# The attention's reciprocal: a power on GpSimd instead of logarithm, exponential and Newton step

## The chip, the core and the metric

The kernel runs on one core of a Trainium2 chip. The core has five engines that run side by side and meet through semaphores: TensorE (PE; its weight loads are shown as PEld), VectorE (DVE), ScalarE (ACT), GpSimd (POOL) and SyncE (SP), which issues nearly all transfers here. Every engine works through its own instructions in a fixed order. The metric is device time in microseconds (us) from the first to the last instruction, with what lies around it.

## The reference

One encoder layer is applied to two requests, a prompt of 1024 tokens and a sample of 256, each behind 16 learned meta tokens. The input is normalised and projected by one matrix of 2048 x 6656; the strips of 128 columns are queries, keys, values and gates of 16 heads. Eight heads attend to all tokens (two heads of keys and values for the eight), eight to a neighbourhood and the meta tokens. Each head's output is multiplied by a gate, and one matrix of 2048 x 2048 projects the result back. The part that the change touches is the softmax:

```
s = jnp.einsum('blkgd,bskd->bkgls', qg, k).astype(jnp.float32) * scale
p = jax.nn.softmax(s, axis=-1).astype(v.dtype)
o = jnp.einsum('bkgls,bskd->blkgd', p, v)
...
ya = global_gqa(qa, ka, va) * jax.nn.silu(za)
```

The softmax divides each exponential by the sum over the keys. The kernel divides at the end: it sums the products of unnormalised exponentials and values, and multiplies by the gate and by one over the sum.

## The kernel before, in words

All matrix products are made of three passes in a reduced 32-bit format: each operand is split into a high part (a cast on ACT, L52) and a low part (a subtraction on DVE, L53), and high x high, high x low and low x high are added in PSUM.

The work has three stages. The first chunk (`chunk1`) projects 512 tokens (meta, sample and the first 240 of the prompt) strip by strip in `strips` (L178 to L180) and does the attention of the sample: 16 blocks of 256 queries, one per head. The second chunk (`chunk2`) projects the other 784 tokens and does the attention of the prompt: 32 wide blocks (`attend`: 256 queries against all 1024 keys, L300 to L302 for the scores and L340 to L343 for the values), and 32 narrow ones (`attend_strip`: L405 to L407 and L436 to L439). The last narrow blocks lie beside the first steps of the output projection (`outproj`, `products`, L887 to L889).

A block goes like this. Keys lie along the partitions, queries along the free dimension. PE makes the scores; ACT and DVE copy them to SBUF and take the running maximum (L304 to L315); `all_max` adds the meta scores (L250) and has POOL take the maximum over the partitions (`ma`, L252); DVE subtracts it (L320), ACT takes the exponential (L321), both split it for PE; `all_sum` adds up (L267), and POOL sums over the partitions (`tot`, L269): afterwards each of the 128 partitions holds the same 256 sums. PE multiplies by the values into `po`. Then `put_y` makes `y`: the reciprocal `r` of `tot` (L276 to L279), `po` times the gate (L282 or L285), that times `r` (L286), and the store to `yd` from SP (L287). The product with the gate, which frees the one PSUM buffer of `po`, doesn't need `r`.

POOL's other work is the sum over the partitions for the queries' and keys' norms (`m`, L188 in `qk_evac`), which the evacuation of a projected strip waits for. Four PSUM buffers (`pp`) hold projected strips.

Between the blocks the projections run on: the next heads' strips, and strips for the narrow heads that are done ahead (`fill`). The order in which each engine takes its instructions is written out when the kernel is built, by a planner that simulates the program and issues what is ready by priority (`TileContext(..., schedule_with_timeline_sim=True)`); weight loads have a raised priority (`woff`) and run ahead, in rings of three raw and four split buffers. Only after the attention, from step 8 of `outproj`, the order is that of the program (`in_order`). At run time the order is fixed: an instruction that waits holds all that stands behind it on its engine.

The reciprocal before is an estimate and one Newton step: exp(-ln(tot)) on ACT, then on DVE `tot * r`, and `(tot * r - 2) * r`, which is minus the refined reciprocal; the sign is taken back in L286 by a factor of -1.

Of the kernel before, what the change touches and what calls it, by code (L numbers as in the profile page):

```python
# [12 lines left out]
F32 = mybir.dt.float32  # L13
F32R = mybir.dt.float32r
AF = mybir.ActivationFunctionType
ALU = mybir.AluOpType
# [4 lines left out]
P = 128  # L21
# [13 lines left out]
QB = 256  # L35
# [10 lines left out]
class Kern:  # L46
# [225 lines left out]
    def put_y(self, po, tot, zs, ydst):  # L272

        nc = self.nc
        r = self.t.tile([P, QB], F32, tag="t", name="r")
        nc.scalar.activation(r[:], tot[:], AF.Ln)  # L276
        nc.scalar.activation(r[:], r[:], AF.Exp, scale=-1.0)
        nc.vector.tensor_tensor(out=tot[:], in0=tot[:], in1=r[:], op=ALU.mult)
        nc.vector.scalar_tensor_tensor(out=r[:], in0=tot[:], scalar=2.0, in1=r[:], op0=ALU.subtract, op1=ALU.mult)  # L279
        y = self.y.tile([P, QB], F32, tag="y", name="y")  # L280
        if len(zs.shape) == 3:
            nc.vector.tensor_tensor(out=y[:].rearrange("p (g r) -> p g r", g=4), in0=po[:].rearrange("p (g r) -> p g r", g=4),  # L282
                                    in1=zs, op=ALU.mult)
        else:
            nc.vector.tensor_tensor(out=y[:], in0=po[:], in1=zs, op=ALU.mult)  # L285
        nc.vector.scalar_tensor_tensor(out=y[:], in0=y[:], scalar=-1.0, in1=r[:], op0=ALU.mult, op1=ALU.mult)  # L286
        nc.sync.dma_start(ydst, y[:].rearrange("p (g r) -> p g r", g=4) if len(ydst.shape) == 3 else y[:])  # L287

    def attend(self, q, zs, keys, meta, vals, vmeta, ydst):
# [700 lines left out]
    def build(self):  # L990
        tc, nc, io = self.tc, self.nc, self.io
        self.woff = 300
        nc.scalar.preload_act_table_set("natural_log_exp_and_others")
        with tc.tile_pool(name="dr", bufs=1, space=DRAM) as dp, tc.tile_pool(name="const", bufs=1) as cp, \
                tc.tile_pool(name="raw", bufs=3) as self.raw, tc.tile_pool(name="w", bufs=4) as self.w:
            self.kd = [dp.tile([P, 2, NMETA + C1P], F32, name=f"kd{g}") for g in range(10)]
            self.vn = [dp.tile([NP, P], F32, name=f"vn{g}") for g in range(10)]
            self.vmd = [dp.tile([M3, P], F32, name=f"vmd{g}") for g in range(10)]
            self.qd = [dp.tile([P, 2, C1P], F32, name=f"qd{h}") for h in range(16)]
            self.zd = [dp.tile([P, NP], F32, name=f"zd{h}") for h in range(16)]  # L1000
            self.k2d = [dp.tile([P, T2], F32, name=f"k2d{g}") for g in range(10)]
            self.q2d = [dp.tile([P, T2], F32, name=f"q2d{h}") for h in range(16)]
            self.yd = [dp.tile([P, NP + NS], F32, name=f"yd{h}") for h in range(16)]
            self.x2d = [dp.tile([P, T2], F32, name=f"x2d{k}") for k in range(KT)]
            self.wld = [dp.tile([P, KT, P], F32, name=f"wld{c}") for c in range(52)]
            self.td = [{p: dp.tile([P, 8, P], F32, name=f"td{c}_{p}") for p in (5, 6, 7, 4)} for c in range(8)]
            self.ident = cp.tile([P, P], F32, name="ident")
            make_identity(nc, self.ident)
            self.nw = cp.tile([P, KT], F32, name="nw")
            self.nqkw = cp.tile([P, 4], F32, name="nqkw")  # L1010
            self.qkw = cp.tile([P, 4], F32, name="qkw")
            with ExitStack() as ps, ExitStack() as es_y:
                def pool(stack, name, bufs, **kw):
                    setattr(self, name, stack.enter_context(tc.tile_pool(name=name, bufs=bufs, **kw)))

                for name, bufs in (("sp", 2), ("op", 1), ("tp", 1)):
                    pool(ps, name, bufs, space=PSUM)
                es_pp, es_x, es_attn, es_proj, es_late = (ExitStack() for _ in range(5))
                kw = {"reuse_waits": "tile"}
                pool(es_pp, "pp", 4, space=PSUM)  # L1020
                pool(ps, "mt", 1)
                self.meta_tiles()
                work = (("s", 5), ("ph", 2), ("sm", 2), ("mx", 2), ("t", 6))
                raw = self.raw
                with ExitStack() as es_1:
                    pool(es_1, "x", 16, side="right")
                    for name, bufs in (("raw", 5), ("tab", 1), ("k", 1), ("v", 1), *work, ("y", 2), ("one", 1), ("ev", 9), ("xr", 10)):
                        pool(es_1, name, bufs)
                    self.chunk1()
                self.raw = raw  # L1030
                pool(es_x, "x", 16, side="right", **kw)
                for name, bufs in (("one", 1), ("ev", 8)):
                    pool(es_proj, name, bufs, side="right", **kw)
                for name, bufs in (("k", 1), ("v", 1), ("tab", 1), ("q", 1), ("z", 1), *work, ("y", 1)):
                    pool(es_attn, name, bufs, **kw)
                self.chunk2()
                es_proj.close()
                es_x.close()
                es_pp.close()
                pool(es_y, "pq", 2, space=PSUM, **kw)  # L1040
                for name, bufs in (("ym", 16), ("us", 8)):
                    pool(es_late, name, bufs, side="right", **kw)
                self.raws, self.ws = [self.raw] * 2, [self.w] * 2

                def end_attention():
                    es_attn.close()
                    for name, bufs in (("yr", 4), ("ysp", 1), ("w2", 4), ("raw2", 4), ("vs", 8), ("ob", 3)):
                        pool(es_y, name, bufs, **kw)
                    self.raws[1], self.ws[1] = self.raw2, self.w2
                    self.ysum = [self.ysp.tile([P, TH], F32, tag=f"ys{k}", name="ysum") for k in range(8)]  # L1050

                self.outproj(end_attention)
                es_late.close()
# [70 lines left out]
```

## Time and profile before

| | us |
|---|---|
| three runs, median | 2243.62 (2240.49 to 2244.88) |
| the profiled execution | 2239.06 |
| its span, first to last instruction | 2237.3 |
| busy: PE | 2203.6 |
| busy: DVE | 1636.4 |
| busy: ACT | 1128.8 |
| busy: POOL | 524.8 |

The profile is that of one execution, taken by the hardware profiler. A group row reads: line, engine, operation, tiles written and read, shape, count, then the busy time in us and the mean duration in ns, and behind the second bar the idle time of the engine just before, and what ended it. A row of the timeline reads: start and duration in us, engine, line, operation, tiles, count, and in brackets the idle time before. A row of a stage reads: its bounds and length, the busy time (and number) of each engine, the granted TensorE clock as a share of full speed, the share of the transfer engines, and GB/s.

### The profile page before, as it was taken

The page shows a single profiled execution, that of the slowest core. Times are in us where ns is not written, and L with a number is a line of the kernel's source. Part 1 is how long each engine was busy: PE and PEld are TensorE (multiplying, and loading weights), DVE is VectorE, ACT ScalarE, POOL GpSimd, SP SyncE. Part 2 cuts the span into 40 slices and gives each one's busy share as a digit, 9 for nine tenths or more (in the row PEclk, how much of TensorE's full clock was granted, in tenths as well). Part 3 has the DMA queues.
Part 4 walks back from the last instruction along what each step waited for, and adds up shares of the span by engine and source line. Part 5 has one row for each costly group of instructions (what it writes and reads, how often), then busy time and mean ns, then how long its engine had stood idle before and what let it go on. Part 6 is the DMA issues. An engine that isn't in the chain of part 4 may idle for free.

```text
span 2237.3 us, 36770 instructions
## 1 busy us (share of the span) xinstructions
PE 2203.6 (98%) x13074; PEld 2091.4 (93%) x13074; DVE 1636.4 (73%) x2895; ACT 1128.8 (50%) x2297; POOL 524.8 (23%) x249
## 2 busy tenths in 40 slices
PE   8999999999969999999999999999999999999999
PEld 7888788888869999999999999999999999999999
DVE  8687876677665899886898889767668776636743
ACT  6555544444464667665666666444344454232220
POOL 1232421222102243221233223323223312000000
PEclk9999999999989999999999999999999999999999
DMA  8767899976454333334333345644334464845663
GB/s 295 218 193 229 288 328 335 300 237 199 137 189 131 104 110 110 104 109 138 105 105 103 106 120 159 201 150 144 116 114 132 134 200 146 262 145 162 201 209 111
DMA packets 262873, 384.80 MB, mean 172 GB/s; under 512 B 46208, under 2 KB 121888, under 8 KB 262688
## 3 DMA queue, kind: packets, MB, share of 16 engines
q1 hardware_dynamic: 262688, 382.44, 54.2%
q8 instruction: 103, 1.69, 0.3%
q14 instruction: 82, 0.67, 0.1%
HBM read 279.77 MB, written 102.42 MB: 171 GB/s over the span
## 4 chain that ended last, share of the span: by engine, by line
PE 86%; DVE 6%; DMA 4%; ACT 2%; issue 1%; POOL 1%; SPq 0%; DVEq 0%; POOLq 0%; ACTq 0%
PE pp L179 18%; PE pp L180 18%; PE pp L178 18%; PE pq L887 6%; PE pq L889 6%; PE pq L888 6%; PE po L439 2%; PE sp L300 1%; PE sp L302 1%; PE sp L301 1%; PE po L342 1%; PE po L341 1%; PE po L340 1%; DVE wl L53 1%; DMA wld<-wl 1%
## 5 line engine op out<-in xcount | busy, mean ns | idle before, releaser
L179 PE MATMUL pp<-x,wh 128*128 128x392 f32 (+2 forms) x2496 | 894.5, 359 | 10.6 <-DVE x L130 10.6
L178 PE MATMUL pp<-x,wh 128*128 128x392 f32 (+2 forms) x2496 | 893.9, 359 | 5.9 <-ACT wh L52 5.9
L180 PE MATMUL pp<-x,wl 128*128 128x392 f32 (+2 forms) x2496 | 892.1, 358 | 0.2 <-DVE wl L53 0.2
L179 PEld LDWEIGHTS pp<-x,wh 128*128 128x128 f32 x2496 | 470.2, 188 | 42.7 <-DVE x L130 11.1
L178 PEld LDWEIGHTS pp<-x,wh 128*128 128x128 f32 x2496 | 469.5, 188 | 38.7 <-ACT wh L52 7.3
L180 PEld LDWEIGHTS pp<-x,wl 128*128 128x128 f32 x2496 | 470.1, 188 | 32.8 <-DVE wl L53 1.2
L53 DVE TENSOR_TENSOR wl<-wr,wh 128x512 fp32r<-128x512 f32 (+1 forms) x402 | 291.1, 736 | 141.9 <-ACT wh L52 94.4
L52 ACT CAST wh<-wr 128x512 fp32r<-128x512 f32 (+1 forms) x402 | 239.7, 609 | 228.7 <-PE pp L179 168.8
L188 POOL PARTITION_ALL_REDUCE m<-ms x78 | 227.1, 2911 | 362.9 <-ACT ms L186 327.8
L269 POOL PARTITION_ALL_REDUCE tot<-a x80 | 188.4, 2354 | 459.6 <-DVE a L267 436.6
L888 PE MATMUL pq<-ym,wh 128*128 128x320 f32 x896 | 277.4, 310 | 0.3 <-DVE ym L53 0.3
L889 PE MATMUL pq<-ym,wl 128*128 128x320 f32 x896 | 277.4, 310 | 0.0
L887 PE MATMUL pq<-ym,wh 128*128 128x320 f32 x896 | 277.2, 310 | 0.0
L252 POOL PARTITION_ALL_REDUCE ma<-m x80 | 100.7, 1259 | 460.8 <-DVE m L250 458.4
L888 PEld LDWEIGHTS pq<-ym,wh 128*128 128x128 f32 x896 | 168.4, 188 | 0.6 <-DVE ym L53 0.6
L887 PEld LDWEIGHTS pq<-ym,wh 128*128 128x128 f32 x896 | 168.2, 188 | 0.1
L889 PEld LDWEIGHTS pq<-ym,wl 128*128 128x128 f32 x896 | 168.4, 188 | 0.0
L320 DVE TENSOR_TENSOR S<-S,ma 128x512 f32<-128x512 f32 x136 | 105.4, 830 | 8.8 <-POOL ma L252 8.5
L53 DVE TENSOR_TENSOR pl<-S,ph 128x512 fp32r<-128x512 f32 x136 | 98.0, 727 | 13.4 <-ACT ph L52 13.0
L59 ACT ACTIVATE rs_l<-m 128x392 f32<-128x392 f32 (+2 forms) x78 | 43.9, 562 | 126.7 <-DVE m L189 125.1
L304 ACT COPY S<-sp 128x512 f32<-128x512 f32 x136 | 78.1, 578 | 51.4 <-PE sp L302 38.9
L321 ACT ACTIVATE S<-S 128x512 f32<-128x512 f32 x136 | 83.9, 629 | 39.7 <-DVE S L320 39.3
(207 smaller groups left out, 3338.1 us busy)
## 6 DMA issues: line engine op xcount, KB each, us to landing
wr<-in_w_in SPq DMA_DIRECT2D x414, 256.0 KB
wld<-wl SPq DMA_DIRECT2D x132, 256.0 KB
wl<-wld SPq DMA_DIRECT2D x132, 256.0 KB
wq<-in_w_out SPq DMA_DIRECT2D x64, 256.0 KB
td<-wq SPq DMA_DIRECT2D x64, 256.0 KB
wr<-td SPq DMA_DIRECT2D x64, 256.0 KB
yr<-yd SPq DMA_DIRECT2D x48, 320.0 KB
wr<-in_w_out SPq DMA_DIRECT2D x48, 256.0 KB
```

The source lines that it names most:

```text
L52: nc.scalar.copy(hi, full)
L53: return nc.vector.tensor_tensor(out=lo, in0=full, in1=hi.bitcast(F32), op=ALU.subtract).ins
L178: nc.tensor.matmul(p[:, :n], wh[:, k, :], xh[:, o:o + n], start=first, stop=False)
L179: nc.tensor.matmul(p[:, :n], wh[:, k, :], xl[:, o:o + n], start=False, stop=False)
L180: nc.tensor.matmul(p[:, :n], wl[:, k, :], xh[:, o:o + n], start=False, stop=last)
L188: nc.gpsimd.partition_all_reduce(m2[:], ms[:], P, RED.add)
L252: nc.gpsimd.partition_all_reduce(ma[:], m1[:], P, RED.max)
L269: nc.gpsimd.partition_all_reduce(tot[:], a1[:], P, RED.add)
L320: nc.vector.tensor_tensor(out=s, in0=s, in1=mb, op=ALU.subtract)
L887: nc.tensor.matmul(ps[:, b, :B], wh, yh[:, o], start=k == 0, stop=False)
L888: nc.tensor.matmul(ps[:, b, :B], wh, yl[:, o], start=False, stop=False)
L889: nc.tensor.matmul(ps[:, b, :B], wl, yh[:, o], start=False, stop=k == 7)
```

## The change

The reciprocal becomes one instruction on POOL: `tot` to the power of -1, where the exponents come from a new constant column `m1` of -1.0 that is read again for each of the 256 columns. The two ACT passes and the two DVE passes of the estimate and the Newton step go. Since `r` now has its true sign, the last multiplication is a plain product of two tensors on DVE. All 80 blocks use `put_y`.

```diff
         nc = self.nc
         r = self.t.tile([P, QB], F32, tag="t", name="r")
-        nc.scalar.activation(r[:], tot[:], AF.Ln)
-        nc.scalar.activation(r[:], r[:], AF.Exp, scale=-1.0)
-        nc.vector.tensor_tensor(out=tot[:], in0=tot[:], in1=r[:], op=ALU.mult)
-        nc.vector.scalar_tensor_tensor(out=r[:], in0=tot[:], scalar=2.0, in1=r[:], op0=ALU.subtract, op1=ALU.mult)
+        nc.gpsimd.tensor_tensor(out=r[:], in0=tot[:], in1=self.m1[:].to_broadcast([P, QB]), op=ALU.pow)
         y = self.y.tile([P, QB], F32, tag="y", name="y")
...
             nc.vector.tensor_tensor(out=y[:], in0=po[:], in1=zs, op=ALU.mult)
-        nc.vector.scalar_tensor_tensor(out=y[:], in0=y[:], scalar=-1.0, in1=r[:], op0=ALU.mult, op1=ALU.mult)
+        nc.vector.tensor_tensor(out=y[:], in0=y[:], in1=r[:], op=ALU.mult)
         nc.sync.dma_start(ydst, y[:].rearrange("p (g r) -> p g r", g=4) if len(ydst.shape) == 3 else y[:])
...
             make_identity(nc, self.ident)
+            self.m1 = cp.tile([P, 1], F32, name="m1")
+            nc.gpsimd.memset(self.m1[:], -1.0)
```

## The prediction

> **What bounds the kernel now.** I read the page first: the engines' busy time and the chain that ended last.
>
> ```profile
> span 2237.3 us, 36770 instructions
> PE 2203.6 (98%) x13074; PEld 2091.4 (93%) x13074; DVE 1636.4 (73%) x2895; ACT 1128.8 (50%) x2297; POOL 524.8 (23%) x249
> ...
> PE 86%; DVE 6%; DMA 4%; ACT 2%; issue 1%; POOL 1%; SPq 0%; DVEq 0%; POOLq 0%; ACTq 0%
> ```
>
> TensorE (PE) is busy for 2203.6 of 2237.3 us, so at most 33.7 us could be won by taking work off the other engines. What matters is whether the edit makes PE wait. The next view is the busy time by stage: the 16 small attention blocks of the first chunk (88 to 634 us), two runs of 16 wide blocks (`attend`, one per group of heads, 740 to 1056 and 1080 to 1396), and the narrow blocks (`attend_strip`, 1396 to 1890).
>
> ```profile
> core 0: us, PE busy (x) PEld busy (x) DVE busy (x) ACT busy (x) POOL busy (x), PEclk, DMA share, GB/s
> 88.00:634.00 546.00, 536.98 (x2535) 446.21 (x2533) 393.27 (x673) 266.63 (x537) 147.27 (x56) 1.00 0.77 247
> 740.00:1056.00 316.00, 316.00 (x2052) 315.11 (x2051) 274.02 (x494) 207.06 (x430) 88.45 (x43) 1.00 0.38 111
> 1080.00:1396.00 316.00, 315.31 (x2059) 312.47 (x2058) 283.90 (x515) 209.47 (x438) 99.74 (x48) 1.00 0.38 116
> 1396.00:1890.00 494.00, 492.68 (x3074) 491.06 (x3074) 357.43 (x724) 230.74 (x499) 150.37 (x82) 1.00 0.46 145
> ```
>
> PE has no gap in any of the attention stages. VectorE (DVE) is the next fullest: 274.0 of 316 us (87%) in the wide stage, 72% elsewhere. The third view is POOL (GpSimd) in order of time, in the wide stage.
>
> ```profile
> 1083.37 1.06 POOL L252 PARTITION_ALL_REDUCE ma<-m  x1 [0.58 <-DVE m L250]
> 1096.30 1.79 POOL L269 PARTITION_ALL_REDUCE tot<-a  x1 [11.86 <-DVE a L267]
> 1100.50 1.06 POOL L252 PARTITION_ALL_REDUCE ma<-m  x1 [2.42 <-DVE m L250]
> ```
>
> The blocks run one behind the other, 17.1 us apart here: the reduction for the maximum (`ma`), 11.9 us of exponentials and sums, the reduction for the sum (`tot`), and 2.4 us after its end the next block's `ma`. The new power reads `tot`, so it lands in exactly that short gap of POOL. And the chain of waits, in order of time, goes through `ma` in this stage:
>
> ```profile
> 1134.74 2.73 POOL ma L252
> 1137.49 4.01 DVE S L320 x4
> ```
>
> So a late `ma` there is not covered: PE's work is in a fixed order, and the next score and value products stand in it.
>
> **The change, part by part.** Removed from each of the 80 calls of `put_y`: two ACT passes and two DVE passes.
>
> ```profile
> L279 DVE SCALAR_TENSOR_TENSOR r<-tot,r 128x256 f32<-128x256 f32 x80 | 35.5, 444 | 1.3
> ...
> L278 DVE TENSOR_TENSOR tot<-tot,r 128x256 f32<-128x256 f32 x80 | 34.8, 435 | 28.0 <-ACT r L277 27.1
> ...
> L276 ACT ACTIVATE r<-tot 128x256 f32<-128x256 f32 x80 | 33.3, 416 | 84.8 <-POOL tot L269 84.5
> L277 ACT ACTIVATE r<-r 128x256 f32<-128x256 f32 x80 | 33.2, 415 | 1.7
> ```
>
> That frees 33.3 + 33.2 = 66.5 us of ACT and 35.5 + 34.8 = 70.3 us of DVE (0.88 us a block). Neither is what PE waits for, so I count the gain as 0. L286 stays with a plainer opcode and the same operands: 0. The memset of `m1` happens once, like the `vm` memset of 0.2 us at the start: 0.
>
> Added: 80 powers of 128x256 on POOL, an operation that no row shows. The nearest rows are POOL's plain passes:
>
> ```profile
> L488 POOL MEMSET Pm<- x2: 314/316/317, 0.9 to 1.1; 128x256 f32 x2
> ```
>
> ```profile
> 9.79 1.23 POOL masks.py:199 TENSOR_SCALAR_AFFINE_SELECT ident<-ident 128x128 f32<-128x128 f32 x1 [8.22 <-issue]
> ```
>
> One pass over 128x256 costs 0.316 us if it only writes; the select, which tests and chooses, costs 1.23 us for half the elements, 2.46 us for all. A full-precision power is a logarithm, a product and an exponential. If POOL does these by arithmetic and not by a table, I count some 32 steps (split off the exponent 3, polynomial 8, product in two words 6, split off the integer 2, second polynomial 6, put the exponent back 2, special values 5). At one pass each that is 32 x 0.316 = 10.1 us, the price I take: the operation is nearer to a string of passes than to a single one. The ends: 2.5 us (the select) below, and 64 passes or 20 us above.
>
> [...] No run here shows a two-input POOL pass.
>
> What waits: DVE's `y` multiply (L286) waits for the power, and behind it on DVE stand the splits of weights, the projections' evacuations and the next block's maximum; the `yd` store (L287) waits on SP with the weight loads and rope shuffles behind it. The weights are loaded ahead and hide it; the maximum and the shuffles are part of the same lateness that I charge now. POOL itself runs in order, so `ma` and the projections' reductions (L188) start only when the power is done. How much of the 10.1 us fits in the gaps, from POOL's groups in the wide stage (x16), the narrow one (x31) and the first chunk (two rows):
>
> ```profile
> L252 POOL PARTITION_ALL_REDUCE ma<-m x16 | 20.4, 1277 | 53.1 <-DVE m L250 53.1
> ```
>
> ```profile
> L252 POOL PARTITION_ALL_REDUCE ma<-m x31 | 37.6, 1212 | 133.3 <-DVE m L250 130.9 <-DMA wr<-in_w_in 2.2
> ```
>
> ```profile
> L188 POOL PARTITION_ALL_REDUCE m<-ms x24 | 79.3, 3302 | 115.9 <-ACT ms L186 91.6 <-DMA wld<-wl 10.3 <-DMA wr<-in_w_in 7.9
> L252 POOL PARTITION_ALL_REDUCE ma<-m x16 | 21.5, 1341 | 225.1 <-DVE m L250 225.1
> ```
>
> - Wide: 53.1 / 16 = 3.3 us idle before `ma` (where a reduction L188 comes first, that one is late instead). Each block is late by 10.1 - 3.3 = 6.8 us; 32 x 6.8 = 218 us.
> - Narrow: 133.3 / 31 = 4.3 us idle; late by 5.8 us. Here PE comes later to the value product than its input is ready:
>
> ```profile
> 1494.95 0.41 ACT L261 CAST Pm<-Sm 48x256 fp32r<-48x256 f32 x1
> ```
>
> ```profile
> 1499.31 0.34 PE L178 MATMUL pp<-x,wh 128*128 128x392 f32 x1
> 1499.49 0.34 PE L179 MATMUL pp<-x,wh 128*128 128x392 f32 x1
> 1499.66 0.38 PE L460 MATMUL tp<-ident,vt 128*128 128x128 f32 x2
> 1499.80 0.36 PE L436 MATMUL po<-Pm,vm 128*128 128x256 f32 x1
> ```
>
>   The probabilities end at 1495.36, the product starts at 1499.80: 4.4 us of cover. 32 x (5.8 - 4.4) = 45 us.
> - First chunk: 225.1 / 16 = 14.1 us idle before `ma`, more than 10.1: 0. A reduction L188 has 115.9 / 24 = 4.8 us; late by 5.3 us, 16 x 5.3 = 85 us at most. I take 0, since four PSUM buffers stand between it and PE, and keep 85 for the range.
> - Clock: after the idle stretch at the change of chunks PE ran at half clock (0.55 in the mean of the first window), with 0.33 us from matmul to matmul where the rows at 1499 us have 0.18.
>
> ```profile
> 649.03 0.53 PE L180 MATMUL pp<-x,wl 128*128 128x392 f32 x1
> 649.36 0.53 PE L179 MATMUL pp<-x,wh 128*128 128x392 f32 x1
> ```
>
> ```profile
> 648.00:652.00 4.00, 3.46 (x12) 3.46 (x13) 4.00 (x7) 3.18 (x9) 0.00 (x0) 0.55 0.00 0
> 652.00:656.00 4.00, 4.00 (x24) 4.00 (x24) 4.00 (x6) 1.89 (x4) 0.00 (x0) 1.00 0.00 0
> ```
>
>   Up to 3.4 us at half clock lose 1.7 us per long stall; for half of the 32 wide blocks 16 x 1.7 = 27 us.
>
> Sum: the profiled execution took 2239.06 us (the median of the runs is 4.6 us higher, 0.2%); 2239 + 218 + 45 + 27 = 2529, forecast **2530 us**. With a power of 6 us it is 2239 + 32 x 2.7 = 2325; with 13 us, 2239 + 32 x 9.7 + 32 x 4.3 + 27 = 2714.
>
> **The rivals.**
>
> *The power is short and fits in the gap* (the other side). It decides at 3.3 us. For it: the select at 2.46 us for all elements. Against: the select does one test, the power dozens of steps. Then nothing is late, and the freed DVE and ACT time can only shorten PE's 33.7 us of waits, mostly at the change of chunks: 2236 us.
>
> *The power also holds DVE.* DVE passes with two inputs in SBUF are held while a POOL reduction runs; those with one input in PSUM never are:
>
> ```profile
> L320 DVE TENSOR_TENSOR S<-S,ma x136: 675/684/2669, 95.0 to 1373.1; 128x512 f32<-128x512 f32 x136
> ```
>
> ```profile
> L310 DVE TENSOR_TENSOR mx<-mx,sp x64: 666/680/691, 736.6 to 1362.4; 128x512 f32<-128x512 f32 x64
> ```
>
> ```profile
> 366.49 3.24 POOL L188 PARTITION_ALL_REDUCE m<-ms  x1 [7.87 <-DMA wr<-in_w_in]
> ```
>
> ```profile
> 366.64 3.39 DVE L510 TENSOR_TENSOR wq<-wq 128x512 f32<-128x512 f32 x2
> ```
>
> L320 (two in SBUF) reaches 2669 ns, L310 (one in PSUM) never passes 691; two passes at L510 took 3.39 us inside a 3.24 us reduction. If a power holds DVE for its whole 10.1 us, DVE is the bound: 274 - 14 + 16 x 10.1 = 422 us of work in a wide stage of 316, so +106, and +116 in the second; 357 - 27 + 31 x 10.1 = 643 in 494 narrow, +149; in the first chunk 541 fits in 546. 2239 + 371 + 27 = 2637 us, and 2870 us at 13 us a power. Against: a reduction held L510 for only about 2 of its 3.24 us, and the power may read its input early.
> [...]
>
> *The power is far dearer*: 20 us, or code fetched at each switch from reduction to power (POOL sat 8.22 us in "issue" before its first select; no reduction shows that). 32 x 16.7 + 32 x 11.3 + 16 x 5.9 + 54 = 1044, so 3283 us.
>
> **How the numbers follow.** Forecast (power 6 to 13 us, POOL's queue late) 0.50, its own range 2325 to 2715; power between 3.3 and 6 us, 2240 to 2325, 0.06; short power 0.12; DVE held 0.24; far dearer 0.08. Leaving out the short and the far dearer power (0.20 together), and taking in the 85 us of the first chunk and DVE held with 13 us, the range is 2270 to 3000. A measurement of this kernel can tell about 0.2%, 4.5 us, from no change. Only the short power gives that: within 0.2% 0.09, faster 0.03, slower 0.88.
>
> **What would show it.** In the profile after: the duration of the new POOL group (10 us; under 3.3 us the forecast falls); `ma` starting right behind the power in the wide stage; PE below 95% busy between 740 us and the end of the wide blocks, with waits on DVE and ACT at L300 and L340, and a granted clock under 1.0 there. If L320 or L53 lengthen to the power's own duration, the held DVE is right. If the power is long and PE still full, the wide blocks had cover that I did not see.

## The result, and the profile after

The changed kernel takes 5911.74 us (median of 4 runs, 5909.94 to 5913.47); the kernel before took 2242.09 us beside it (4 runs, 2240.49 to 2244.88). The ratio is 2.636, with a 95% interval of 2.632 to 2.641. The forecast was 2530 us in a range of 2270 to 3000: the direction was right, the size was not, and even the dearest rival (3283 us) stayed far below.

The page of the changed kernel: busy time, three rows of tenths in 40 slices, and the chain that ended last.

```profile
span 5910.1 us, 36754 instructions
...
PE 2458.6 (42%) x13074; PEld 2293.3 (39%) x13074; DVE 1587.8 (27%) x2735; ACT 1094.4 (19%) x2137; POOL 3777.6 (64%) x330
...
PE   9353545667414261414323665456010100100399
...
POOL 3767656556766676666666767777767677776500
PEclk9676777878657685657666777778555555555699
...
POOL 27%; PE 9%; issue 8%; DVE 3%; POOLq 1%; ACT 1%; DMA 0%; SPq 0%; DVEq 0%; ACTq 0%
```

PE falls from 98% busy to 42%, and POOL is the fullest engine with 64%. In the last third of the attention PE works for less than a tenth of most slices. Only the last two slices, the output projection without a reciprocal, look as before. The chain names POOL first, and next to PE something that it calls "issue": time in which the engine waited for nothing that the profile shows. The costliest groups of the same page say who waits:

```profile
L276 POOL TENSOR_TENSOR r<-tot,m 128x256 f32<-128x256 f32 x80 | 3296.8, 41210 | 593.9 <-issue 482.9
...
L283 DVE TENSOR_TENSOR y<-y,r 128x256 f32<-128x256 f32 x80 | 34.0, 425 | 2725.5 <-POOL r L276 2725.5
L433 PE MATMUL po<-Pm,vm 128*128 128x256 f32 x32 | 17.7, 552 | 1509.1 <-DVE Pm L262 1179.0
...
L337 PE MATMUL po<-ph,va 128*128 128x256 f32 x256 | 102.6, 401 | 1220.8 <-ACT ph L52 1220.8
```

(The lines of code after `put_y` stand three lower than before.) One power takes 41.2 us. That alone is four times the price in the forecast. Behind the bar stand 593.9 us of idle POOL time in front of the 80 powers, 7.4 us each, most of it (482.9 us) put down to "issue". PE waits in the value products of the narrow blocks (1509.1 us) and the wide ones (1220.8 us), for probabilities that come late. One wide block on POOL, in order of time:

```profile
1368.51 2.17 POOL L269 PARTITION_ALL_REDUCE tot<-a  x1 [10.95 <-DVE a L267]
1377.71 41.17 POOL L276 TENSOR_TENSOR r<-tot,m 128x256 f32<-128x256 f32 x1 [7.04 <-issue]
1424.90 1.08 POOL L252 PARTITION_ALL_REDUCE ma<-m  x1 [6.01 <-issue]
1425.90 2.65 POOL L188 PARTITION_ALL_REDUCE m<-ms  x1
1438.05 1.79 POOL L269 PARTITION_ALL_REDUCE tot<-a  x1 [9.51 <-DVE a L267]
```

The blocks are 69.5 us apart (1368.51 to 1438.05) where they were 17.1. There is a hole of 7.0 us ahead of the power and one of 6.0 us behind it, though the sum was there, and the next maximum's input too, since 1371.74 us by DVE's timeline:

```profile
1371.33 0.41 DVE L250 TENSOR_TENSOR m<-m,Sm 16x256 f32<-16x256 f32 x1
```

What stands in these holes is in the list of all the instructions that line 276 gave POOL and its sequencer (count, then duration in ns: least, median, most):

```profile
L276 POOLq MODIFY_POOL_CONFIG  x160: 87/88/88, 108.0 to 5513.3; - x160
L276 POOL TENSOR_TENSOR r<-tot,m x80: 41172/41172/41813, 115.7 to 5524.1; 128x256 f32<-128x256 f32 x80
```

Ahead of each power stand two instructions that by their name change POOL's configuration (MODIFY_POOL_CONFIG), and ahead of the reduction behind it two more (122 at L252, 34 at L188, 2 at L138). They last 0.1 us each at most, but a hole of 6 to 7 us follows them (the first starts at 108.0 us, the first power at 115.7); what fills it the profile doesn't show. So a power costs 7.4 + 41.2 + 6.0 = 54.6 us of POOL, and 80 of them 4368 us. In the kernel before there are four such instructions in the whole program, two at 1.6 us and two at 11.2 us.

The stages, between two landmarks that both kernels have: the first wide block's `ma`, and the last `tot`. First the kernel before, a row of POOL's timeline and one of the list of L269:

```profile
743.57 1.06 POOL L252 PARTITION_ALL_REDUCE ma<-m  x1 [0.58 <-DVE m L250]
```

```profile
L269 POOL PARTITION_ALL_REDUCE tot<-a x80: 1793/2092/5072, 100.9 to 1883.6; - x80
```

Then the same two rows of the changed kernel:

```profile
1356.23 1.33 POOL L252 PARTITION_ALL_REDUCE ma<-m  x1 [1.24 <-DVE m L250]
```

```profile
L269 POOL PARTITION_ALL_REDUCE tot<-a x80: 1794/1872/3453, 104.6 to 5511.5; - x80
```

| | before | after | difference |
|---|---|---|---|
| start to the first wide `ma` | 743.6 | 1356.2 | +613 |
| first wide `ma` to the last `tot` | 1140.0 | 4155.3 | +3015 |
| last `tot` to the end | 353.7 | 398.6 | +45 |

### The profile page after: what moved, and what is told of

Same layout as the page of the kernel before. It is cut to its first block, busy times and chain, and to the rows that moved or that the text cites. A ratio compares the mean times of both kernels' runs of the same rounds, so it can differ in the third digit from the quotient of the medians.

```text
span 5910.1 us, 36754 instructions
## 1 busy us (share of the span) xinstructions
PE 2458.6 (42%) x13074; PEld 2293.3 (39%) x13074; DVE 1587.8 (27%) x2735; ACT 1094.4 (19%) x2137; POOL 3777.6 (64%) x330
## 5 line engine op out<-in xcount | busy, mean ns | idle before, releaser
L276 POOL TENSOR_TENSOR r<-tot,m 128x256 f32<-128x256 f32 x80 | 3296.8, 41210 | 593.9 <-issue 482.9
L178 PE MATMUL pp<-x,wh 128*128 128x392 f32 (+2 forms) x2496 | 915.8, 368 | 321.3 <-DVE rs_r L204 301.2
L179 PE MATMUL pp<-x,wh 128*128 128x392 f32 (+2 forms) x2496 | 912.7, 366 | 2.5 <-DVE x L130 2.5
L180 PE MATMUL pp<-x,wl 128*128 128x392 f32 (+2 forms) x2496 | 907.0, 364 | 0.2 <-DVE wl L53 0.2
L283 DVE TENSOR_TENSOR y<-y,r 128x256 f32<-128x256 f32 x80 | 34.0, 425 | 2725.5 <-POOL r L276 2725.5
L433 PE MATMUL po<-Pm,vm 128*128 128x256 f32 x32 | 17.7, 552 | 1509.1 <-DVE Pm L262 1179.0
L178 PEld LDWEIGHTS pp<-x,wh 128*128 128x128 f32 x2496 | 483.6, 194 | 361.9 <-issue 283.6
L337 PE MATMUL po<-ph,va 128*128 128x256 f32 x256 | 102.6, 401 | 1220.8 <-ACT ph L52 1220.8
L337 PEld LDWEIGHTS po<-ph,va 128*128 128x128 f32 x256 | 73.8, 288 | 1229.8 <-ACT ph L52 1229.6
L179 PEld LDWEIGHTS pp<-x,wh 128*128 128x128 f32 x2496 | 483.8, 194 | 36.0 <-DVE x L130 2.7
L269 POOL PARTITION_ALL_REDUCE tot<-a x80 | 160.6, 2008 | 396.4 <-DVE a L267 396.4
L252 POOL PARTITION_ALL_REDUCE ma<-m x80 | 88.4, 1105 | 492.4 <-issue 353.5
L188 POOL PARTITION_ALL_REDUCE m<-ms x78 | 225.9, 2896 | 264.1 <-ACT ms L186 136.0
L53 DVE TENSOR_TENSOR wl<-wr,wh 128x512 fp32r<-128x512 f32 (+1 forms) x402 | 275.7, 696 | 418.6 <-ACT wh L52 399.3
```

The source lines that it names most:

```text
L53: return nc.vector.tensor_tensor(out=lo, in0=full, in1=hi.bitcast(F32), op=ALU.subtract).ins
L178: nc.tensor.matmul(p[:, :n], wh[:, k, :], xh[:, o:o + n], start=first, stop=False)
L179: nc.tensor.matmul(p[:, :n], wh[:, k, :], xl[:, o:o + n], start=False, stop=False)
L180: nc.tensor.matmul(p[:, :n], wl[:, k, :], xh[:, o:o + n], start=False, stop=last)
L188: nc.gpsimd.partition_all_reduce(m2[:], ms[:], P, RED.add)
L269: nc.gpsimd.partition_all_reduce(tot[:], a1[:], P, RED.add)
```

## The experiments

The first theory: POOL's own queue is late by the price of the power with its changes of configuration. That price has two parts, arithmetic and change, and the experiments take them apart, along with the question of who stands in the queue. Each diff is against the kernel before, unless it says otherwise; the column `m1` is there in all. The times of e6 and e7 are medians of 11 and 4 runs; every other experiment was run once.

**e1_mult: the changes without the arithmetic.** Against the changed kernel:

```diff
-        nc.gpsimd.tensor_tensor(out=r[:], in0=tot[:], in1=self.m1[:].to_broadcast([P, QB]), op=ALU.pow)
+        nc.gpsimd.tensor_tensor(out=r[:], in0=tot[:], in1=self.m1[:].to_broadcast([P, QB]), op=ALU.mult)
```

> The power is replaced by a product of the same two tensors on POOL, so the output lacks the reciprocal. Theory (every plain two-tensor operation between two reductions makes POOL change its code twice, and POOL's queue carries it to PE): the new row falls from 41.2 us to under 1 us, 160 MODIFY_POOL_CONFIG rows stay at it, about 13.6 us of switching a block stays, and by the prediction's formula with a price of 14.2 us the time is 2239 + 32 x 10.9 + 32 x 5.5 + about 40 = 2800 us. Rival (only the power needs other code): no such rows, time 2235 to 2260 us.

Measured: 2928.18 us (the kernel before beside it 2237.88), 128 us above the theory's 2800 and far from its rival. POOL's group for the product:

```profile
L276 POOL TENSOR_TENSOR r<-tot,m 128x256 f32<-128x256 f32 x80 | 48.3, 604 | 615.4 <-issue 562.6 <-DMA wld<-wl 20.6 <-DMA z<-zd 14.2
```

The product takes 0.6 us, and there are 7.7 us of idle time ahead of it all the same. An operation that lasts 0.6 us makes the kernel 690 us slower. The changes of configuration are a price of their own, and the product between the reductions pays it as the power does.

**e2_mult_unread and e3_pow_unread: the same operations, with nobody waiting.** The old reciprocal stays; behind the Newton step POOL overwrites `tot`, which nobody reads any more:

```diff
         nc.vector.scalar_tensor_tensor(out=r[:], in0=tot[:], scalar=2.0, in1=r[:], op0=ALU.subtract, op1=ALU.mult)
+        nc.gpsimd.tensor_tensor(out=tot[:], in0=tot[:], in1=self.m1[:].to_broadcast([P, QB]), op=ALU.mult)   # e3: ALU.pow
```

> The old reciprocal is back; behind it a product on POOL overwrites tot, and nothing reads it. Theory (POOL's queue: the next reductions stand behind the switching): the same lateness as with the product read, 2700 to 2850 us. Rival (the loss comes from DVE, which waits for POOL at the y multiply and holds what stands behind it): nobody waits any more, 2240 to 2350 us.

> The same with the power: the old reciprocal feeds y, and a power that nothing reads follows on POOL. Theory (POOL's queue): 5800 to 5950 us, as with the change. Rival (DVE's wait at the y multiply adds its own part): down to what POOL alone needs, 80 x 54.7 + 476 us of reductions + about 430 us outside the attention = 5280 us.

Measured: 2732.7 us with the product, 5369.5 us with the power. So most of the loss is there without a reader of the result: it comes from POOL's queue, from what stands behind the operation. But e3 missed the theory's 5800 to 5950 us and landed near the rival's floor. POOL's timeline of e3 shows a difference that I hadn't counted on:

```profile
1301.94 1.81 POOL L269 PARTITION_ALL_REDUCE tot<-a  x1 [5.84 <-issue]
1303.66 2.65 POOL L188 PARTITION_ALL_REDUCE m<-ms  x1
1306.21 1.15 POOL L252 PARTITION_ALL_REDUCE ma<-m  x1
1314.66 41.17 POOL L280 TENSOR_TENSOR tot<-tot,m 128x256 f32<-128x256 f32 x1 [7.30 <-DVE rs_r L202]
1362.13 2.57 POOL L188 PARTITION_ALL_REDUCE m<-ms  x1 [6.29 <-issue]
1364.62 1.88 POOL L269 PARTITION_ALL_REDUCE tot<-a  x1
```

Here the planner put the power behind the next block's `ma`, so that the exponentials between that `ma` and its `tot` run beside the power, and `tot` needs no wait of its own. In the changed kernel the power stands right behind its own `tot`, and the next `ma`, exponentials and `tot` come one after the other behind it. Counted over both timelines, the power comes directly behind a `ma` 60 times of 80 in e3, and never in the changed kernel, where it comes directly behind a `tot` 69 times. The 542 us between 5912 and 5370 could be this place, or DVE standing at the multiply that reads the power; the last two runs tell these apart.

**e5_pow64 and e10_pow_half_rows: what the arithmetic is paid by.** In e5 the power does 64 of the 256 columns on all 128 partitions, in e10 all 256 columns on 64 partitions; the rest goes the old way:

```diff
+        c = 64
+        nc.gpsimd.tensor_tensor(out=r[:, :c], in0=tot[:, :c], in1=self.m1[:].to_broadcast([P, c]), op=ALU.pow)
+        nc.scalar.activation(r[:, c:], tot[:, c:], AF.Ln)
...
```

> The power on 64 of the 256 columns, the old way for the other 192. Theory (the price goes by the column, 41.2/256 = 0.161 us each): 10.3 us a power, 23.9 us with the switching, and by the prediction's formula 2239 + 32 x 20.6 + 32 x 15.2 + 16 x 9.8 + 54 = 3595 us. Rival (a fixed price of an instruction): about 41 us a power and 5900 us.

> The power on 64 of the 128 partitions, all 256 columns; the other 64 partitions the old way. Theory (the price goes by the column, whatever the number of partitions): 41.2 us a power, 5800 to 6000 us. Rival (by the element): 20.6 us a power, 34 us with the switching, and by the prediction's formula 2239 + 32 x 30.8 + 32 x 25.4 + 16 x 20 + 54 = 4410 us.

Measured: e5 3564.3 us, e10 5906.81 us. POOL's group of e5, and the list of L277 in e10:

```profile
L277 POOL TENSOR_TENSOR r<-tot,m 128x64 f32<-128x64 f32 x80 | 848.0, 10600 | 610.8 <-issue 474.9 <-DMA wld<-wl 35.5 <-DMA vn<-vl 22.3
```

```profile
L277 POOL TENSOR_TENSOR r<-tot,m x80: 41172/41173/41707, 112.0 to 5518.3; 64x256 f32<-64x256 f32 x80
```

A quarter of the columns takes 10.6 of 41.2 us, half of the partitions takes the same 41.2 us. The power costs 0.161 us for each column (41.17 / 256), with 64 partitions as with 128. And e5, whose arithmetic of 10.6 us is near the price that the forecast took, can be put into the forecast's formula: with 7.6 + 10.6 + 6.0 = 24.2 us it gives 2239 + 32 x 20.9 + 32 x 15.5 + 16 x 10.1 = 3565 us without its clock term.

**e4_pow3: three powers in a row.**

```diff
+        nc.gpsimd.tensor_tensor(out=r[:], in0=tot[:], in1=self.m1[:].to_broadcast([P, QB]), op=ALU.pow)
+        nc.gpsimd.tensor_tensor(out=r[:], in0=r[:], in1=self.m1[:].to_broadcast([P, QB]), op=ALU.pow)
+        nc.gpsimd.tensor_tensor(out=r[:], in0=r[:], in1=self.m1[:].to_broadcast([P, QB]), op=ALU.pow)
```

> Three powers in a row instead of one (the reciprocal of the reciprocal of the reciprocal). Theory (a switch comes with each change between reduction and plain operation, not with each power): still 160 MODIFY_POOL_CONFIG rows at the power's lines, a price of 3 x 41.2 + 13.5 = 137 us a block, and by the prediction's formula 2239 + 32 x 133.7 + 32 x 128.3 + 16 x 123 + 54 = 12650 us. Rival (each power brings its own switches): 480 rows and over 14700 us.

Measured: 12885.45 us, 2% above the theory's number, but not by the theory's order. The lists of the three lines show 4, 158 and 158 configuration instructions ahead of the powers, 320 where 160 were expected. POOL's timeline tells why:

```profile
3104.32 1.81 POOL L269 PARTITION_ALL_REDUCE tot<-a  x1 [5.75 <-issue]
3113.52 41.17 POOL L278 TENSOR_TENSOR r<-r,m 128x256 f32<-128x256 f32 x1 [7.40 <-issue]
3154.69 41.11 POOL L276 TENSOR_TENSOR r<-tot,m 128x256 f32<-128x256 f32 x1
3201.56 1.08 POOL L252 PARTITION_ALL_REDUCE ma<-m  x1 [5.76 <-issue]
```

One block's third power (L278) and the next block's first (L276) stand back to back, without a hole; the others have a reduction between them. So the hole belongs to the alternation of reduction and elementwise operation, not to the power: two of a kind in a row pay nothing. That the total met the expectation is chance. With two pairs of changes a block the price is 3 x 41.2 + 2 x 13.4 = 150.4 us, and the formula gives 2239 + 32 x 147.1 + 32 x 141.7 + 16 x 136.3 = 13661 us, 6% too much. In e4 POOL hardly waits for anything else: its busy time on the page, 10343.7 us, and 160 pairs of holes at 13.4 us make 12488 of the 12885 us.

**e6_none and e7_dve_recip: what the removed passes are worth.** e6 multiplies by `tot` itself and has no reciprocal at all; e7 has one reciprocal instruction on DVE:

```diff
-        (the two activations, the product and the Newton step)
+        nc.vector.reciprocal(out=r[:], in_=tot[:])      # e7; nothing in e6
```

> No reciprocal at all: the two ACT and two DVE passes go and nothing comes instead, y is multiplied by tot itself, so the output lacks the reciprocal. Theory (the removed passes were beside PE's work, gain 0): 2235 to 2245 us. Rival (they cost PE something): under 2230 us.

> DVE's own reciprocal, one instruction, in place of the power. A candidate for a version better than both. It keeps POOL free; DVE has 0.88 us a block less of the old passes and one reciprocal more, of unknown duration. Theory (what counts is whether PE waits): with 2 us or less DVE still fits in the wide stage (274 - 14 + 32 = 292 of 316 us), 2235 to 2260 us. Rival (DVE's order is tight in the wide stage, so each us more is late there): 32 x 1.2 = 38 us more, 2280 us.

Measured: e6 2242.99 us, a ratio to before of 1.0012 (1.0003 to 1.0021); e7 2261.35 us, 1.0098 (1.0082 to 1.0113). Without any reciprocal the kernel is not faster, so by this run another way of making it has nothing to gain. The reciprocal on DVE takes 1.75 us, twice the two passes that it replaces there, and costs 1%, a little more than its theory's 2260 us:

```profile
L276 DVE RECIPROCAL r<-tot 128x256 f32<-128x256 f32 x80 | 139.8, 1748 | 30.0 <-POOL tot L269 30.0
```

**e8_y_on_pool and e9_mult_y_on_pool: the reader moved to POOL.** If DVE's wait at the last multiply were what costs, POOL could do that multiply itself. e8 against the changed kernel; e9 is the same with e1's product for the power:

```diff
-        nc.vector.tensor_tensor(out=y[:], in0=y[:], in1=r[:], op=ALU.mult)
+        nc.gpsimd.tensor_tensor(out=y[:], in0=y[:], in1=r[:], op=ALU.mult)
```

> As the change, but the last multiplication by r is on POOL, right behind the power: DVE no longer waits for the power, and POOL has one more plain product (0.6 us) a block, with no further switch. Theory (of the time of the change, what the unread power took away, 5912 - 5370 = 542 us, is DVE's queue standing behind that multiplication): 5370 + 80 x 0.6 = 5420 us, 5350 to 5500. Rival (it is the old reciprocal being placed elsewhere by the planner, or y being late): 5850 to 5980 us.

> The same with the product in place of the power (the output lacks the reciprocal). Theory (DVE's queue): the 195 us between the product that is read and the one that isn't go, 2733 + 48 = 2780 us, 2700 to 2830. Rival: 2900 to 3000 us.

Measured: e8 6546.01 us, e9 3338.88 us. Both are above both theories, so they do not decide the question. POOL's timeline of e8 shows what got in the way:

```profile
1556.75 1.08 POOL L252 PARTITION_ALL_REDUCE ma<-m  x1 [6.04 <-issue]
1557.75 2.65 POOL L188 PARTITION_ALL_REDUCE m<-ms  x1
1567.70 0.73 POOL L283 TENSOR_TENSOR y<-y,r 128x256 f32<-128x256 f32 x1 [7.30 <-issue]
1574.32 1.81 POOL L269 PARTITION_ALL_REDUCE tot<-a  x1 [5.90 <-issue]
```

The multiply was placed behind the next reductions and not behind the power, and pays a second pair of changes. The lists count 160 configuration instructions ahead of the powers (in e9, the products) and these ahead of the multiplies, in e8 and in e9:

```profile
L283 POOLq MODIFY_POOL_CONFIG  x158: 87/98/98, 167.0 to 6131.9; - x158
```

```profile
L283 POOLq MODIFY_POOL_CONFIG  x82: 88/98/98, 184.3 to 2965.9; - x82
```

That is 79 more pairs of holes in e8 and 41 in e9, at some 13.4 us: 1059 and 549 us, of which 634 (6546 - 5912) and 411 us (3339 - 2928) show in the time. A multiply of 0.73 us has cost 634 / 80 = 7.9 us a block.

**e11_pow_late_read and e12_mult_late_read: place or reader.** As e3 and e2, but the result is read: `y` is multiplied by it once more on DVE, which stands and waits as in the changed kernel. The diff is that of e11; in e12 the product by -1 takes up the sign, and the multiply by `r` ahead of it is a plain product.

```diff
         nc.vector.scalar_tensor_tensor(out=r[:], in0=tot[:], scalar=2.0, in1=r[:], op0=ALU.subtract, op1=ALU.mult)
+        nc.gpsimd.tensor_tensor(out=tot[:], in0=tot[:], in1=self.m1[:].to_broadcast([P, QB]), op=ALU.pow)   # e12: ALU.mult
...
         nc.vector.scalar_tensor_tensor(out=y[:], in0=y[:], scalar=-1.0, in1=r[:], op0=ALU.mult, op1=ALU.mult)
+        nc.vector.tensor_tensor(out=y[:], in0=y[:], in1=tot[:], op=ALU.mult)
```

> The old reciprocal, then the power of the refined product (about 1) in place on POOL, as in e3_pow_unread, but now read: y is multiplied by it once more on DVE. In POOL's order the power stands as in e3, mostly behind the next block's maximum or another reduction; in the changed kernel it stands right behind its own block's sum. Theory that the difference between 5912 and 5370 us is the place in POOL's order: near e3, 5370 to 5480 us. Rival, that it is DVE's queue standing behind the multiply that waits for the power: near the changed kernel, 5800 to 5950 us.

> The same with a product by -1 in place of the power (the sign is taken up by the last multiply). e1, with the short pass read, took 2928 us; e2, with it unread, 2733 us. Place in POOL's order: near e2, 2710 to 2800 us. DVE's queue: near e1, 2880 to 2960 us.

Measured: e11 5448.42 us, e12 2763.83 us; both near the kernels without a reader. The row for the reader in DVE's waits of e11 (us in total, times, longest), and POOL's order there:

```profile
DVE y L288 <- POOL tot L280: 2248.6, 78, 46.7
```

```profile
1304.03 1.15 POOL L252 PARTITION_ALL_REDUCE ma<-m  x1
1312.30 41.24 POOL L280 TENSOR_TENSOR tot<-tot,m 128x256 f32<-128x256 f32 x1 [7.12 <-DVE rs_r L202]
1359.68 2.57 POOL L188 PARTITION_ALL_REDUCE m<-ms  x1 [6.14 <-issue]
```

DVE waits 2248.6 us for the power, not far from the 2725.5 us in the changed kernel, yet the kernel is 463 us faster, with the power behind `ma` as in e3 (58 times of 80). POOL's own wait shows the place: ahead of `tot` it stands idle for DVE's sum `a`, which the exponentials feed, 396.4 us in the changed kernel (its group row) and 44.5 us in e11 (from the list of L269):

```profile
L269 POOL PARTITION_ALL_REDUCE tot<-a x80 | 160.6, 2008 | 396.4 <-DVE a L267 396.4
```

```profile
  DVE a L267: 44.5, 16
```

So of the 542 us 463 go with the place in POOL's order and 79 with the reader; for the short product it is 164 and 31 us of 195. There the place differs in a part of the blocks only: the product comes directly behind a `ma` 34 times of 80 in e2, 29 in e12, and never in e1. The runs carry other changes of the planner's order with them, so these are sizes, not exact parts.

## Why the prediction was wrong, point by point

- **What bounds the kernel, and that the gain is 0: right.** e6 leaves the whole reciprocal out and gains nothing (ratio 1.0012).
- **The price of the power: this is the step that failed.** The forecast took "32 x 0.316 = 10.1 us", 32 passes at the price of a memset's. Measured are 41.2 us of arithmetic, and 13.4 us of configuration changes that the forecast's price left out: 54.6 us, 5.4 times as much. A memset only writes, and the count of 32 steps was my own estimate; no row of the profile carried either, and no run shows it. The upper end of 20 us came from the same guess, so it was no bound. A row 130 times shorter than the answer can be "the nearest row" and still say nothing.
- **The changes of configuration: named, and given a chance of 0.08.** The row that showed them was quoted: the select's 8.22 us in "issue". That the reductions showed no such hole was read as evidence that switching is rare; it only meant that the kernel before changes at its start alone: two instructions ahead of the select (1.6 us), two ahead of the first reduction (11.2 us), and none between its blocks. And the rival was written as a dear power *or* changes, so that even its 3283 us had room for only one of the two. Both came together.
- **The formula for what is late: right in kind; its size holds at the change's price and less well at small ones.** With 54.6 us in place of 10.1 it gives 32 x (54.6 - 3.3) = 1642 us wide, 32 x (54.6 - 8.7) = 1469 us narrow, and 16 x (54.6 - 14.1) = 648 us in the first chunk. The table above has +613 us up to the first wide block (formula 648), and +3060 us from there on (formula 3111). The sum without a clock term is 2239 + 3759 = 5998 us, 1.5% above the 5912 measured. At e1's price, 7.7 + 0.6 + 6.0 = 14.3 us, it gives 2239 + 352 + 179 + 3 = 2773 us and is 5% short of 2928. The next table has the lateness of one block in us by stage: for the wide and the narrow blocks the stretch from the first `ma` to the last, less the same stretch before, by its 31 steps; for the first chunk the stretch up to the first wide `ma`, by 16. (The stretches before are 743.57 to 1366.68 and 1384.06 to 1878.07 us; in the changed kernel 1356.23 to 3511.91 and 3585.71 to 5507.09.)

| | changed kernel, formula | measured | e5, formula | measured | e1, formula | measured |
|---|---|---|---|---|---|---|
| first chunk | 40.5 | 38.3 | 10.1 | 11.9 | 0.2 | 8.6 |
| wide | 51.3 | 49.4 | 20.9 | 19.3 | 11.0 | 9.5 |
| narrow | 45.9 | 46.0 | 15.5 | 16.1 | 5.6 | 7.9 |

  In the changed kernel the formula holds stage by stage. That it met e5's time within 0.1% is partly luck, since its errors have both signs there; and e1's 5% come from the first chunk, 138 us later where the formula has 3, and from the narrow blocks.
- **The first chunk at 0: wrong, and not by the price alone.** The 14.1 us of idle time were there; 54.6 us pass them. But the forecast also put the lateness of the projections' reduction (L188), 85 us at most, at 0, because four PSUM buffers stand between it and PE. In the changed kernel's first chunk the largest of PE's waits is the one for the evacuation behind that reduction, and before there was none (us in total, times, longest):

```profile
PE pp L178 <- DVE rs_r L204: 290.0, 10, 47.7
```

  In e1's first chunk it is ACT that stands longer for the norm behind this reduction, 191.3 us ahead of L59 where it was 54.7; how much of the 138 us comes by this way no run separates.
- **`ma` right behind the power: right, at a distance of 6 us.** This was the test named in advance, and it shows the mechanism: the next maximum stands in POOL's queue and not in DVE's, since DVE had written its input by 1371.74 us and `ma` started at 1424.90. e3 and e11 add what the forecast didn't see, that the place of the power in that queue is worth 463 us.
- **The rival that the power holds DVE: wrong.** DVE's timeline inside the power that ran from 1377.71 to 1418.88 us:

```profile
1372.59 0.42 DVE L282 TENSOR_TENSOR y<-po,z 128x256 f32<-128x256 f32 x1
1393.73 0.57 DVE L197 TENSOR_TENSOR t<-t,rope 128x392 f32<-128x392 f32 x1 [20.72 <-DMA ts<-t]
1394.21 0.56 DVE L198 TENSOR_TENSOR ts<-ts,rope 128x392 f32<-128x392 f32 x1
1394.81 0.57 DVE L199 TENSOR_TENSOR t<-t,ts 128x392 f32<-128x392 f32 x1
1418.92 0.43 DVE L283 TENSOR_TENSOR y<-y,r 128x256 f32<-128x256 f32 x1 [23.55 <-POOL r L276]
```

  Three passes with both inputs in SBUF run in 0.57 us each in the middle of the power. DVE then stands for 23.55 us at the multiply that needs the power's result, which is a wait for a value. Nor does L320 (now L317), which the forecast named as the sign, lengthen to a power's duration anywhere: its longest is 2.69 us, where it was 2.67.

```profile
L317 DVE TENSOR_TENSOR S<-S,ma x136: 676/683/2687, 98.7 to 3516.4; 128x512 f32<-128x512 f32 x136
```

  By its own terms, this rival's time at 13 us a power comes to 2860 us and not to 2870. The prediction's rows show passes held by a reduction (L320 at 2669 ns, least 675); the trace shows no such hold by the power, with 0.57 us inside 41.17 us.
- **The clock: right in direction, its size not settled.** The granted clock in the stages of the changed kernel (the column after the busy times):

```profile
88.00:1290.00 1202.00, 633.42 (x2803) 529.27 (x2802) 429.05 (x704) 298.97 (x565) 791.31 (x72) 0.74 0.37 119
1300.00:3560.00 2260.00, 961.99 (x5261) 926.41 (x5261) 612.76 (x1055) 480.86 (x959) 1501.74 (x135) 0.70 0.14 43
3560.00:5570.00 2010.00, 443.26 (x2381) 433.54 (x2381) 306.91 (x628) 179.00 (x372) 1468.01 (x110) 0.59 0.10 31
5570.00:5910.00 340.00, 334.32 (x2262) 333.71 (x2262) 177.35 (x248) 81.89 (x138) 0.00 (x0) 0.99 0.56 174
```

  It was 1.00 in every attention stage before. The forecast's 3.4 us at half clock was an estimate from one restart (first matmul at 648.54 us, clock 1.00 from 652). Behind the power of 1377.71 us the granted clock is 0.50 from 1419 us on; PE starts again at 1430.06 us, with 0.54 still between 1435 and 1436 us and 1.00 from there, so 3.4 us was no upper bound. PE's busy time grows from 2203.6 to 2458.6 us for the same 13074 matmuls, 255 us, against 27 in the forecast. How much of that lies in the waits for POOL anyway no run separates; the sum above is met without it.
- **Rising from the product to the power.** Before to e2, the product unread: +495 us. To e1, with the product right behind the sum and read: +195 us. To the changed kernel, with the power for the product: +2984 us, of 80 x 40.6 = 3248 us of added arithmetic. The changes of configuration and a short product alone make the kernel 31% slower (e1).

What stays open: what fills the holes behind the configuration instructions; what makes the first chunk 138 us later at a price of 14 us, where the formula has 3; and whether the planner would give the power a better place in the changed kernel with another duration for it, which no run tried. A version that beats the kernel before was not found on this path, and e6 shows no gain to look for.

## What to carry to other kernels

Before an operation is moved to an engine that the profile has never shown doing it, look for two prices: that of the operation itself, for which a write-only pass is no measure (0.316 us here, beside 41.17), and that of changing between it and what this engine already does (13.4 us a block here). An unexplained "issue" hole ahead of the one instruction of a new kind in a profile can be such a price, and here it was paid at each alternation, not once. And count first what the removed work is worth: here nothing, so the best that could be expected was no change, and every unknown price could only lose.

## What the runs showed of the hardware that was not expected

- An elementwise power on GpSimd takes 0.161 us for each column, 41.17 us for 256, with 128 partitions as with 64 (e10). A product of the same shape takes 0.60 us (e1), 68 times less.
- A change between GpSimd's partition reductions and its plain two-input operations (power and product) costs about 7.4 us ahead of the operation (7.7 in e1) and 6.0 us ahead of the reduction, each time, 80 and 79 times in the changed kernel. Two powers in a row pay nothing (in e4 one ends and the next starts at 3154.69 us), nor do two reductions (in the changed kernel `ma` runs from 1424.90 us for 1.08 us, and `m` starts at 1425.90). What fills the holes no run shows.
- While a power runs, DVE's passes with two inputs in SBUF keep their 0.57 us (L197's median in the kernel before: 570 ns), though the prediction's rows showed such passes held during a reduction (2669 against 675 ns for L320).
